# Order of the partial products in the projections: all sixteen matmuls with the weights' first parts, then the eight with the second parts

## The chip, the cores and the metric

The kernel runs on one core of a Trainium2 chip. The metric is the time of one execution on the device in microseconds (us). Five engines work at the same time, each through a queue of its own in order: TensorE (PE in the rows, its weight loads PEld), VectorE (DVE), ScalarE (ACT), GpSimd (POOL) and SyncE (SP), which here starts transfers.

## What is computed

Two layers of a decoder over 320 tokens (256 of a prompt, 64 of eight samples), model width 1024, all in fp32:

```python
for l in range(DEPTH):
    xn = rmsnorm(x)
    u = xn @ w_in[l]        # IN_WIDTH columns: pooling, its gate z, latents, q/k/v, their gates, 3 branch gates
    A = pool_mixer(...)     # windows 2, 4, 8, 16; mean minus token, then a linear map per group
    B = attention(...)      # latent, over cached pages
    C = gated_delta(...)    # short convolutions, then a chunked recurrence
    x += w_out( sum_b sigmoid(gate_b) * P_b(branch_b * silu(z_b)) )
```

(shortened). Nearly all of the work of TensorE is the product of `xn` with 128 columns of `w_in` at a time.

## The kernel before

Everything is stored with features on the partitions, so that one product gives 128 columns for all 320 tokens: eight steps k of 128 features each, added up in one PSUM tile.

**Three matmuls per step.** For precision each weight tile and `xn` are split in two parts. `split_w` has ScalarE round the weight tile to `wh` (L200) and VectorE, or in some turns GpSimd, subtract to get the rest `wl` (L201). `xn` has the parts `xnH` and `xnL`, made once per layer. A product is then `wh xnH + wh xnL + wl xnH`: 3 matmuls for each of 8 steps, 24 in all. `mm3` (L213 to L226) issues them. It has two forms: steps one after the other with the three matmuls of each together (L223 to L226), or first the sixteen matmuls that use `wh` (L218, L219) and then the eight that use `wl` (L221). Before the change the second form is taken only by the first two products of layer 0.

**Who calls it.** `proj` (L425 to L430) makes a product of the projections into a PSUM tile named `pj`, of which there are two. The rows name it `pj`; a thin product of 72 columns per layer is named `pj` as well. `gate_mm` (L456) makes those of the branch gates (`gate`); it always hands over a range of k, `ks`, which is `(0, 8)` unless a product is issued in pieces. Products of the branches (`br`) have four steps, those of the attention's queries three. The products with `w_out` (`wo`, L1544) have eight and hand over no range.

**Weights.** Raw tiles of 128 x 1024 values come from memory into four buffers (`wraw`); `wh` and `wl` have two buffers each, used in turns. So ScalarE can make the next `wh` when the last matmul that reads the buffer is done.

**Order.** Outside the attention the program is given to a scheduler that places the instructions of every engine by a model of their durations. So the order on VectorE, ScalarE and GpSimd is not that of the code, and moves when products are issued otherwise. Each engine then keeps that order.

**The stretches around the end of a layer's recurrence.** `pooling(g)` makes a product of the pooling branch, its sums `us` over windows (L642), the difference `d` (L646 to L649) and its linear map, a matmul into `mix` (L651); a transpose `pout` (L636) is taken from it as well. `pool_gate(g)` makes the product of its gate: `z` (L658), a tanh `th` (L660, L661). At the same time the delta rule runs on VectorE: a recurrence in seven rounds on `X8` and `R` (L764 to L766), from it three matrices `TS` (L772), which are transposed (L774) and then doubled up in levels: products `Y` (L797) on TensorE, copied by ScalarE (`Yb`, L800), products `Z` (L813), subtracted (L819) and transposed (L820) on VectorE. In layer 1 a logarithm and an exponential on ScalarE (L549, L550) stand behind the first `Yb`; VectorE needs them for `qq` (L552).

Of the kernel before, what the change touches and what calls it, by code (L numbers as in the profile page):

```python
# [36 lines left out]
PRM, RNB, STB, XT, WLP = "M", "M", "M", ("A", "B"), 2  # L37
# [79 lines left out]
def trunk(tc, I, O, layers=2):  # L117
# [66 lines left out]
    turn, hold, pair, paired = [0], [], [0], [1]  # L184
# [28 lines left out]
    def mm3(out, w, x, nk, first=0, ks=None):  # L213
        wh, wl = w
        xh, xl = x
        if l == 0 and turn[0] <= WLP:
            for k in range(nk):
                nc.tensor.matmul(out, wh[:, k, :], xh[:, first + k, :], start=k == 0, stop=False)  # L218
                nc.tensor.matmul(out, wh[:, k, :], xl[:, first + k, :], start=False, stop=False)  # L219
            for k in range(nk):  # L220
                nc.tensor.matmul(out, wl[:, k, :], xh[:, first + k, :], start=False, stop=k == nk - 1)  # L221
            return
        for k in range(*(ks or (0, nk))):  # L223
            nc.tensor.matmul(out, wh[:, k, :], xh[:, first + k, :], start=k == 0, stop=False)  # L224
            nc.tensor.matmul(out, wh[:, k, :], xl[:, first + k, :], start=False, stop=False)  # L225
            nc.tensor.matmul(out, wl[:, k, :], xh[:, first + k, :], start=False, stop=k == nk - 1)  # L226
# [187 lines left out]
    for l in range(layers):  # L414
# [10 lines left out]
        def proj(col):  # L425

            w = split_w(ahead.pop(0) if ahead else load_w(I["w_in"][l][:, col : col + 128], 8, 128), 8)
            b = ps(chunk.get("tag", "pj"), "pj")
            mm3(b[:, :T], w, xn, 8)
            return b[:, :T]  # L430
# [25 lines left out]
        def gate_mm(tag, w, b=None, ks=(0, 8)):  # L456
            b = b or ps(tag, "gate")
            mm3(b[:, :T], w, xn, 8, ks=ks)
            return b
# [102 lines left out]
        w = split_w(small, 8, lambda w: w[:, :, :72])  # L562
        bs = ps("pj", "pj")
        mm3(bs[:72, :T], [i[:, :, :72] for i in w], xn, 8)
        kr4 = per.tile([128, T], F32, name="kr4", tag="kr4")
        tt(kr4[0:32, :], bs[0:32, :T], rn[0:32, :], mult)
# [1041 lines left out]
```

## Time and profile before

| | before |
|---|---|
| median of 3 runs | 1044.32 us (1042.73 to 1047.79) |
| the profiled execution | 1044.8 us, of which the span from first to last instruction is 1042.8 |
| mean granted clock of TensorE | 0.973 of full |
| busy: TensorE | 987.6 us (95%) |
| busy: VectorE | 712.1 us (68%) |
| busy: ScalarE | 466.5 us (45%) |
| busy: GpSimd | 332.2 us (32%) |

The rest of the page is read best by stretches, since the shares of busy time differ between them. In the rows below, `x` behind a busy time is a number of instructions, and `[1.05 <-ACT wh L200]` behind an instruction says that its engine was idle for 1.05 us before it, and that the instruction of line 200 on ScalarE which wrote `wh` released it.

### The profile page before, as it was taken

Reading aid. Unit: us, or ns where it says so; the run is one execution under the profiler, and the core shown is the slowest. Engines: PE = TensorE matmul, PEld = TensorE weight load, DVE = VectorE, ACT = ScalarE, POOL = GpSimd, SP = SyncE. Lnnn points to the kernel's source line nnn. Section 1 sums busy time; section 2 is a strip of 40 time slices with the busy share of each in tenths; the row PEclk is TensorE's granted clock in tenths of the full one; section 3 lists DMA queues with packets and bytes.
Section 4 is the critical chain, followed back from the end, with each engine's and each line's share of the span. In section 5 each row is a group of like instructions: output and inputs, shape, how many; then the busy total and the mean of one; then the engine's idle time right before and its main releaser. Section 6 shows DMA issues by size and latency. Waiting matters only on the chain.

```text
span 1042.8 us, 24809 instructions
## 1 busy us (share of the span) xinstructions
PE 987.6 (95%) x10211; PEld 865.2 (83%) x10211; DVE 712.1 (68%) x1353; ACT 466.5 (45%) x838; POOL 332.2 (32%) x467
## 2 busy tenths in 40 slices
PE   8988899999999999999989979999999999998996
PEld 6877798997878888789978868999887787877996
DVE  3899974658656666677758988646774675754962
ACT  5554253555443333444546534336455333334453
POOL 3656312124250101035445542221334201100631
PEclk8999899999999999999999989999999999999999
DMA  9533324633656776268563333455256577633861
GB/s 235 158 82 101 96 74 111 184 96 91 203 171 202 242 233 225 78 196 233 144 194 94 86 98 82 109 144 140 71 145 232 163 227 259 189 135 126 237 171 51
DMA packets 202698, 159.22 MB, mean 153 GB/s; under 512 B 27704, under 2 KB 191826, under 8 KB 200010
## 3 DMA queue, kind: packets, MB, share of 16 engines
q1 hardware_dynamic: 176364, 98.47, 34.7%
q0 software_dynamic: 7424, 48.75, 13.2%
q10 hardware_dynamic: 18798, 10.44, 3.5%
q8 instruction: 80, 1.31, 0.5%
q14 instruction: 32, 0.26, 0.1%
HBM read 144.17 MB, written 13.68 MB: 151 GB/s over the span
## 4 chain that ended last, share of the span: by engine, by line
PE 73%; DVE 16%; ACT 5%; issue 3%; DMA 2%; POOL 1%; SPq 0%; DVEq 0%; ACTq 0%; POOLq 0%
PE sc L1186 6%; PE pv L1257 6%; PE pj L224 5%; PE gate L224 5%; PE pj L226 5%; PE pj L225 5%; PE gate L226 5%; PE gate L225 4%; DVE cy L509 4%; DVE wl L201 3%; PE br L226 3%; PE br L224 3%; PE br L225 3%; PE wo L224 2%; PE wo L225 2%
## 5 line engine op out<-in xcount | busy, mean ns | idle before, releaser
L201 DVE TENSOR_TENSOR wl<-wraw,wh 128x1024 fp32r<-128x1024 f32 (+2 forms) x169 | 195.9, 1167 | 83.0 <-ACT wh L200 82.0
L200 ACT ACTIVATE wh<-wraw 128x1024 fp32r<-128x1024 f32 (+1 forms) x180 | 166.5, 935 | 156.4 <-PE pj L225 75.8
L224 PE MATMUL pj<-xnH,wh 128*128 128x320 f32 (+1 forms) x528 | 172.7, 327 | 13.0 <-DVE V L501 7.6
L226 PE MATMUL pj<-xnH,wl 128*128 128x320 f32 (+1 forms) x528 | 170.2, 322 | 6.3 <-DVE wl L201 6.0
L225 PE MATMUL pj<-xnL,wh 128*128 128x320 f32 (+1 forms) x528 | 168.6, 319 | 0.0
L224 PE MATMUL gate<-xnH,wh 128*128 128x320 f32 x384 | 125.4, 326 | 1.7 <-DVE V L501 1.5
L226 PE MATMUL gate<-xnH,wl 128*128 128x320 f32 x384 | 121.2, 316 | 2.2 <-DVE wl L201 1.8
L225 PE MATMUL gate<-xnL,wh 128*128 128x320 f32 x384 | 120.1, 313 | 0.0
L224 PEld LDWEIGHTS pj<-xnH,wh 128*128 128x128 f32 (+1 forms) x528 | 101.8, 193 | 19.0 <-ACT wh L200 7.7
L226 PEld LDWEIGHTS pj<-xnH,wl 128*128 128x128 f32 (+1 forms) x528 | 101.7, 193 | 10.6 <-DVE wl L201 7.9
L225 PEld LDWEIGHTS pj<-xnL,wh 128*128 128x128 f32 (+1 forms) x528 | 101.7, 193 | 4.9 <-issue 3.5
L224 PEld LDWEIGHTS gate<-xnH,wh 128*128 128x128 f32 x384 | 73.4, 191 | 9.3 <-issue 5.7
L1176 DVE STREAM_TRANSPOSE KT<-kv 128x1024 f32<-128x1024 f32 x64 | 78.6, 1228 | 0.5
L226 PEld LDWEIGHTS gate<-xnH,wl 128*128 128x128 f32 x384 | 73.3, 191 | 4.0 <-DVE wl L201 2.6
L225 PEld LDWEIGHTS gate<-xnL,wh 128*128 128x128 f32 x384 | 73.5, 191 | 1.1 <-issue 0.8
L224 PE MATMUL br<-yH,wh 128*128 128x320 f32 x192 | 61.1, 319 | 3.0 <-ACT wh L200 2.6
L226 PE MATMUL br<-yH,wl 128*128 128x320 f32 x192 | 60.4, 316 | 1.8 <-DVE wl L201 1.8
L225 PE MATMUL br<-yL,wh 128*128 128x320 f32 x192 | 60.2, 314 | 0.0
L1186 PE MATMUL sc<-KT,q 32*64 32x256 f32 x2048 | 59.3, 377 | 0.0
L1257 PE MATMUL pv<-kv,PT 128*64 128x256 f32 x512 | 58.8, 382 | 0.2
L509 DVE SCALAR_TENSOR_TENSOR cy<-V,prm,cy 128x344 f32<-128x344 f32 x72 | 56.4, 802 | 0.5
L1186 PEld LDWEIGHTS sc<-KT,q 32*64 32x64 f32 x2048 | 45.8, 131 | 12.0 <-issue 5.7
(410 smaller groups left out, 2045.1 us busy)
## 6 DMA issues: line engine op xcount, KB each, us to landing
wraw<-in_w_in SPq DMA_DIRECT2D x114, 512.0 KB
wraw<-in_w_out SPq DMA_DIRECT2D x16, 512.0 KB
q<-q4d SPq DMA_DIRECT2D x64, 72.0 KB
gate<-gt ACTq DMA_DIRECT2D x28, 160.0 KB
gt<-gate POOLq DMA_DIRECT2D x28, 160.0 KB, 3.5
wraw<-in_w_br_pool SPq DMA_DIRECT2D x16, 256.0 KB
wraw<-in_w_br_dn SPq DMA_DIRECT2D x16, 256.0 KB
wraw<-in_w_br_mla SPq DMA_DIRECT2D x16, 256.0 KB
```

The costliest lines, as they stand in the source:

```text
L200: act(h, raw, AF.Copy)
L201: (nc.gpsimd.tensor_tensor if spare or turn[0] in K["lo"] else tt)(lo, raw, h.bitcast(F32), sub)
L224: nc.tensor.matmul(out, wh[:, k, :], xh[:, first + k, :], start=k == 0, stop=False)
L225: nc.tensor.matmul(out, wh[:, k, :], xl[:, first + k, :], start=False, stop=False)
L226: nc.tensor.matmul(out, wl[:, k, :], xh[:, first + k, :], start=False, stop=k == nk - 1)
L509: stt(y, V[:, j : j + 344], wj(j), y, mult, add)
L1176: nc.vector.transpose(v[:, a], kv[:, a * 1024 : a * 1024 + 1024].rearrange("p (i k c) -> p i k c", i=4, k=8))
L1186: nc.tensor.matmul(sc[64 * hf : 64 * hf + 64, g, :256], q4[r, k, :], krT[r, keys_] if k == 8 else KT[r, k, keys_], start=k == 0, stop=k == 8,)
L1257: nc.tensor.matmul(pv[64 * hf : 64 * hf + 64, :256], PT[:, n * 128 + 64 * hf : n * 128 + 64 * hf + 64], kv[:, r : r + 256], start=n == 0, ...
```

## The change

In `mm3` the condition under which the second form is taken becomes: eight steps, and no range of k handed over.

```diff
--- before.py
+++ after.py
@@ -213,7 +213,7 @@
     def mm3(out, w, x, nk, first=0, ks=None):
         wh, wl = w
         xh, xl = x
-        if l == 0 and turn[0] <= WLP:
+        if nk == 8 and not ks:
             for k in range(nk):
                 nc.tensor.matmul(out, wh[:, k, :], xh[:, first + k, :], start=k == 0, stop=False)
                 nc.tensor.matmul(out, wh[:, k, :], xl[:, first + k, :], start=False, stop=False)
```

The two forms make the same 24 matmuls. By the order of the changed program, the products that take the second form are all those named `pj` and the sixteen named `wo`; 82 products more than before. Those named `gate` hand over a range and keep the first form, and so do `br` and the attention's queries.

What TensorE's queue holds in layer 1 for the gate product of a pooling group (pj_7382), before. `pout_7266` is the transpose of the pooling product ahead of it, `wh_7378` and `wl_7379` are its weights:

```order
L224 MATMUL pj_7382<-xnH_113,wh_7378 128x320
L225 MATMUL pj_7382<-xnL_114,wh_7378 128x320
L636 MATMUL pout_7266<-cst_58,u_7264 128x128
L226 MATMUL pj_7382<-xnH_113,wl_7379 128x320
L224 MATMUL pj_7382<-xnH_113,wh_7378 128x320
L225 MATMUL pj_7382<-xnL_114,wh_7378 128x320
L226 MATMUL pj_7382<-xnH_113,wl_7379 128x320
```

And after, from the end of its first sixteen matmuls to the next product (pj_7286):

```order
L636 MATMUL pout_7266<-cst_58,u_7264 128x128
L221 MATMUL pj_7382<-xnH_113,wl_7379 128x320 x8
L651 MATMUL mix_7276<-d_7271,mixw_6292 128x320
L218 MATMUL pj_7286<-xnH_113,wh_7282 128x320
L219 MATMUL pj_7286<-xnL_114,wh_7282 128x320
L218 MATMUL pj_7286<-xnH_113,wh_7282 128x320
L219 MATMUL pj_7286<-xnL_114,wh_7282 128x320
```

All sixteen matmuls with `wh_7378` now stand ahead of the transpose, and the first one with `wl_7379` is the seventeenth, not the third. The mix follows directly on the product in both.

On VectorE at the same place the parts of `d_7271`, the input of that mix, stood together before, between rounds of the recurrence (`X8`, `R`):

```order
L646 SCALAR_TENSOR_TENSOR d_7271<-us_7269,U_7259 128x256
L647 SCALAR_TENSOR_TENSOR d_7271<-us_7269,U_7259 128x64
L766 TENSOR_TENSOR R_7145<-R_7145,X8_7148 128x20x2
L648 TENSOR_TENSOR d_7271<-us_7269,cst1_6413 128x16
L764 STREAM_SHUFFLE X8_7152<-R_7145 128x160
L649 TENSOR_TENSOR d_7271<-d_7271,U_7259 128x16
L765 TENSOR_TENSOR X8_7152<-X8_7152,a8_6603 128x20x3
L766 TENSOR_TENSOR R_7145<-R_7145,X8_7152 128x20x3
L764 STREAM_SHUFFLE X8_7156<-R_7145 128x160
```

After the change:

```order
L646 SCALAR_TENSOR_TENSOR d_7271<-us_7269,U_7259 128x256
L647 SCALAR_TENSOR_TENSOR d_7271<-us_7269,U_7259 128x64
L765 TENSOR_TENSOR X8_7148<-X8_7148,a8_6603 128x20x2
L658 TENSOR_TENSOR z_7407<-pj_7382,rn_112 128x320
L201 TENSOR_TENSOR wl_7491<-wraw_7488,wh_7490 128x1024
L648 TENSOR_TENSOR d_7271<-us_7269,cst1_6413 128x16
L766 TENSOR_TENSOR R_7145<-R_7145,X8_7148 128x20x2
L661 SCALAR_TENSOR_TENSOR th_7409<-th_7409,z_7407 128x320
L649 TENSOR_TENSOR d_7271<-d_7271,U_7259 128x16
```

The gate's `z_7407`, the weights `wl_7491` of a later product and the tanh's `th_7409` moved in between the parts of `d_7271`; before they stood some ten rows further on, behind more rounds. In layer 0 the same three kinds moved in the same way.

Further on in layer 1, VectorE's rows from the end of the recurrence to the two transposes L774, before (`U_7311`, `u_7316`, `us_7321` and `d_7325` belong to the next pooling group):

```order
L766 TENSOR_TENSOR R_7145<-R_7145,X8_7168 128x20x7
L772 TENSOR_TENSOR TS_7172<-R_7145,cst1_6413 128x512
L772 TENSOR_TENSOR TS_7175<-R_7145,cst1_6413 128x512
L772 TENSOR_TENSOR TS_7178<-R_7145,cst1_6413 128x256
L630 TENSOR_TENSOR U_7311<-pj_7286,rn_112 128x256
L631 TENSOR_TENSOR U_7311<-pj_7286,rn_112 128x8x8
L774 STREAM_TRANSPOSE TS_7172<-TS_7172 128x512
L634 TENSOR_TENSOR u_7316<-pj_7286,rn_112 128x128
L774 STREAM_TRANSPOSE TS_7175<-TS_7175 128x512
L201 TENSOR_TENSOR wl_7416<-wraw_7413,wh_7415 128x1024
```

And after:

```order
L766 TENSOR_TENSOR R_7145<-R_7145,X8_7168 128x20x7
L642 TENSOR_TENSOR us_7323<-us_7321 128x452
L772 TENSOR_TENSOR TS_7172<-R_7145,cst1_6413 128x512
L772 TENSOR_TENSOR TS_7175<-R_7145,cst1_6413 128x512
L772 TENSOR_TENSOR TS_7178<-R_7145,cst1_6413 128x256
L658 TENSOR_TENSOR z_7444<-pj_7419,rn_112 128x320
L646 SCALAR_TENSOR_TENSOR d_7325<-us_7323,U_7311 128x256
L647 SCALAR_TENSOR_TENSOR d_7325<-us_7323,U_7311 128x64
L201 TENSOR_TENSOR wl_7589<-wraw_7586,wh_7588 128x1024
L774 STREAM_TRANSPOSE TS_7172<-TS_7172 128x512
L774 STREAM_TRANSPOSE TS_7175<-TS_7175 128x512
```

The transposes had only parts of `U_7311` and `u_7316` ahead of or between them; now `wl_7416` and the first `us` (just ahead of these rows), the second `us`, `z_7444`, two parts of `d_7325` and `wl_7589` stand ahead of both.

TensorE's rows at that place, the products Y that read the transposed matrices, before:

```order
L797 MATMUL Y_7336<-TS_7172,ATm_7334 64x32 x14
L636 MATMUL pout_7318<-cst_58,u_7316 128x128
L797 MATMUL Y_7336<-TS_7172,ATm_7334 64x32 x2
L797 MATMUL Y_7357<-TS_7175,ATm_7355 64x32 x16
L226 MATMUL pj_7419<-xnH_113,wl_7416 128x320
L224 MATMUL pj_7419<-xnH_113,wh_7415 128x320
L225 MATMUL pj_7419<-xnL_114,wh_7415 128x320
```

And after, from the transpose `pout_7318` on:

```order
L636 MATMUL pout_7318<-cst_58,u_7316 128x128
L221 MATMUL pj_7419<-xnH_113,wl_7416 128x320 x8
L797 MATMUL Y_7336<-TS_7172,ATm_7334 64x32 x16
L797 MATMUL Y_7357<-TS_7175,ATm_7355 64x32 x7
L651 MATMUL mix_7330<-d_7325,mixw_6292 128x320
L797 MATMUL Y_7357<-TS_7175,ATm_7355 64x32 x9
L813 MATMUL Z_7450<-Yb_7353,TS_7172 64x32 x16
L813 MATMUL Z_7469<-Yb_7374,TS_7175 64x32 x16
```

Before, Y stood in the middle of the product pj_7419, with `pout_7318` between its parts; now the whole product and `pout_7318` stand ahead of it, and a mix between its parts.

## Rows read from the trace of the kernel before

**Rows 1.** Busy time by stretch: length; busy PE, PEld, DVE, ACT, POOL; PEclk; DMA share; GB/s

```profile
28.00:103.00 75.00, 66.28 (x457) 58.72 (x456) 69.06 (x121) 40.57 (x63) 47.28 (x73) 0.95 0.42 115
103.00:120.00 17.00, 13.09 (x67) 12.15 (x66) 16.21 (x47) 3.70 (x7) 6.32 (x9) 0.80 0.39 107
120.00:240.00 120.00, 118.36 (x1601) 108.37 (x1599) 75.56 (x144) 56.64 (x90) 27.92 (x40) 1.00 0.42 114
...
603.00:624.00 21.00, 14.81 (x80) 13.07 (x80) 18.80 (x48) 6.01 (x9) 10.05 (x13) 0.84 0.38 101
624.00:644.00 20.00, 17.76 (x202) 16.16 (x200) 17.19 (x31) 10.13 (x14) 4.98 (x6) 0.91 0.27 71
644.00:780.00 136.00, 135.24 (x1636) 120.81 (x1636) 88.11 (x169) 62.20 (x105) 36.36 (x46) 1.00 0.44 122
```

**Rows 2.** TensorE's waits over the whole span: us in total, times, longest

```profile
PE pj L224 <- DVE V L501: 7.6, 3, 3.1
PE pj L226 <- DVE wl L201: 6.0, 5, 2.3
PE pj L224 <- ACT wh L200: 3.1, 3, 1.1
...
PE gate L226 <- DVE wl L201: 1.8, 3, 1.1
```

**Rows 3.** Timeline of TensorE, layer 1, 612 to 624 us: start, length, instruction, idle before

```profile
613.37 0.41 PE L224 MATMUL pj<-xnH,wh 128*128 128x320 f32 x1 [1.05 <-ACT wh L200]
...
615.53 0.45 PE L636 MATMUL pout<-cst,u 128*128 128x128 f32 x1 [1.60 <-DVE u L634]
618.33 0.64 PE L226 MATMUL pj<-xnH,wl 128*128 128x320 f32 x1 [2.34 <-DVE wl L201]
618.76 0.47 PE L224 MATMUL pj<-xnH,wh 128*128 128x320 f32 x1
619.03 0.47 PE L225 MATMUL pj<-xnL,wh 128*128 128x320 f32 x1
...
622.90 0.31 PE L226 MATMUL pj<-xnH,wl 128*128 128x320 f32 x1
623.05 0.70 PE L651 MATMUL mix<-d,mixw 128*128 128x320 f32 x2
```

**Rows 4.** Timeline of TensorE, layer 0, 109 to 125 us

```profile
113.98 0.64 PE L226 MATMUL pj<-xnH,wl 128*128 128x320 f32 x1 [1.47 <-DVE wl L201]
...
119.87 0.70 PE L651 MATMUL mix<-d,mixw 128*128 128x320 f32 x2
...
124.03 1.18 PE L797 MATMUL Y<-TS,ATm 64*64 64x32 f32 x34
```

**Rows 5.** Timeline of VectorE, layer 0, 109 to 126 us

```profile
116.12 0.17 DVE L649 TENSOR_TENSOR d<-d,U 128x16 f32<-128x16 f32 x1
...
120.07 0.49 DVE L658 TENSOR_TENSOR z<-pj,rn 128x320 f32<-128x320 f32 x1 [0.49 <-PE pj L226]
```

**Rows 6.** The page's costliest groups: busy, mean ns of one, idle before

```profile
L201 DVE TENSOR_TENSOR wl<-wraw,wh 128x1024 fp32r<-128x1024 f32 (+2 forms) x169 | 195.9, 1167 | 83.0 <-ACT wh L200 82.0
...
L509 DVE SCALAR_TENSOR_TENSOR cy<-V,prm,cy 128x344 f32<-128x344 f32 x72 | 56.4, 802 | 0.5
```

**Rows 7.** Timeline of VectorE, layer 1, 614 to 645 us

```profile
616.43 0.61 DVE L642 TENSOR_TENSOR us<-U 128x454 f32<-128x454 f32 x1
...
619.71 0.17 DVE L649 TENSOR_TENSOR d<-d,U 128x16 f32<-128x16 f32 x1
...
629.66 0.69 DVE L774 STREAM_TRANSPOSE TS<-TS 128x512 f32<-128x512 f32 x1
...
631.38 1.74 DVE L642 TENSOR_TENSOR us<-U 128x454 f32<-128x454 f32 x1
...
638.23 1.70 DVE L552 TENSOR_TENSOR qq<-qq,l 128x320 f32<-128x320 f32 x4 [2.59 <-ACT l L550]
...
643.27 0.71 DVE L820 STREAM_TRANSPOSE TS<-TS 128x512 f32<-128x512 f32 x1
```

## The prediction

> **What bounds the kernel now.** I read busy time by stretch first, then the waits of TensorE, then the timelines of the places where those waits lie. In [rows 1] the reader is to compare PE and DVE in each row. From 28 to 120 us and from 603 to 644 us, the stretches in which layer 0 and layer 1 build their branches, VectorE is the fuller engine: 69.06 of 75, 16.21 of 17, 18.80 of 21 us. From 120 and from 644 us on TensorE is: 118.36 of 120 and 135.24 of 136. So there are two regimes. A wait of TensorE in the first is largely slack, since VectorE would still have to do the same work; only in the second does each microsecond of a product count fully, and there is next to no wait in it to remove.
>
> The list of waits [rows 2] gives those that the change can touch: 6.0 us, five times, for `wl` from VectorE, and 3.1 us, three times, for `wh` from ScalarE (which waits for the last reader of the buffer). Together 9.1 us, 0.9% of the span. The gates' 1.8 us stands there too. The timelines show where the long ones lie. In [rows 3] one product of layer 1 (pj_7382) waits 1.05 us for `wh`, starts, lets a transpose pass that waits 1.60, and then stands 2.34 us at its third matmul for `wl`. Its next matmuls start 0.27 us apart (618.76, 619.03), and the last start 0.15 us apart (622.90 to 623.05): the engine has been granted the lower of its two clock levels (1.2 instead of 2.4 GHz) after those idle pieces, which is what a granted clock of 0.84 and 0.80 in [rows 1] is made of. Layer 0 has the same picture [rows 4]: 1.47 us idle, and the product that started at about 110.7 reaches its end only at 119.87.
>
> **The change part by part.** The sum is made against the profiled execution, 1044.8 us (span 1042.8); the median of the runs is 1044.3, 0.5 below, and I forecast for the median.
>
> *What stays.* No instruction is added or removed; 82 products of 24 matmuls are issued in another order. At 0.15 us per matmul that is 82 x 24 x 0.15 us on either side: 0. The gates pass a range of k in any case, and the order of the changed kernel shows them as before. So the 1.8 us stay.
>
> *What a product gains.* `wl` is needed 14 matmuls later (17th instead of 3rd): 14 x 0.15 = 2.1 us. `wh` is released at the 16th instead of the 23rd: 7 x 0.15 = 1.0 us earlier. That covers four of the five `wl` waits and the three `wh` waits almost wholly, so the upper bound of the gain is 9.1 us, if TensorE were what the end of these stretches waits for. The lower bound is 0, because VectorE is nearer to full there. I take 0 for this term and judge the ends of the two stretches by themselves, since VectorE's order moves with the products.
>
> *End of the stretch in layer 0.* Before, `d` of the mix is ready at 116.12 + 0.17 = 116.3 [rows 5], and the mix stands at 119.87 behind the slow product. Now the product ends about 8 matmuls after its `wl`, near 115 to 116. But its `z` is now ready earlier too, and the scheduler has put `z` (0.49), the next product's `wl` (1.17, [rows 6]) and `th` (about as `z`) between the parts of `d`. With 0.3 of the recurrence that also steps ahead, `d` comes 2.4 us later: 118.7, and the mix at about 119.0, 0.9 earlier than 119.87. The product behind it (24 x 0.15 = 3.6) ends some 0.9 earlier as well, and Y, now at 124.03, by 0.9. But TensorE then idles 3 us in one piece ahead of the mix, where before it lost the clock after 1.47; if half of the next product runs at the lower level that is 12 x 0.12 = 1.4 us back. Bounds -0.9 and +1.4; I take -0.3, near the middle.
>
> *End of the stretch in layer 1.* The same move puts `z`, `wl` and `th` ahead of the last piece of `d`, which before ended at 619.9 [rows 7]: 2.1 us more, so the mix comes near 622.0 instead of 623.05, since its product is no longer late. Then comes the new queue: the two transposes L774, of which the second began at 629.66, now stand behind another `wl` (1.17), a `z` (0.49), two `us` (0.61 each as at 616.43, up to 1.74 as at 631.38), part of `d` (about 0.6) and one more `wl` (1.17). That is 4.6 to 6.9 us more ahead of them. Less the 0.3 by which the earlier product fills an idle piece of VectorE, L774 comes 4.3 us later. Behind it wait Y (TensorE), Yb, then Ln and Exp (ScalarE), then `qq` (L552), which began at 638.23. About 1 us of that chain goes, by my estimate, because a transpose (pout) no longer stands between the parts of Y. So `qq` begins near 641.5 and ends (1.70) near 643.2. But what VectorE used to do behind `qq` (`z`, `wl`, `th`, one pair of L819 and L820) is already done by then; only one pair is left (0.71, and a subtraction on 256 columns, about 0.4 by the 0.49 of `z` on 320), and the last L820 ends near 644.3, against 643.27 + 0.71 = 643.98. Half of the Y that follows needs only the first pair and can run ahead of it, which is worth what the 0.3 costs. So the wait moves from `wl` to Y and nothing is won. Bounds: -1.1 (that pair in no one's way) and +2.3 (both `us` at the long duration, 2 x 1.13). I take 0.
>
> *Other moves.* In layer 1 a convolution's V (L501) stands behind one more `cy` (0.80) and one more `wl` (1.17, [rows 6]), where TensorE already waits up to 3.1 us [rows 2]. In layer 0 a V stands about as much ahead. Bounds -1 and +2, opposite signs in the two layers: 0. The sixteen products of `w_out` lie in a stretch where no wait is listed: 0.
>
> Sum: -0.3 on 1044.8 is 1044.5, or **1044.0** for the median of the runs.
>
> On a rule of the Trainium skill (Perfetto Trace Analysis, Optimization Strategies): keep the matmul engine as full as the program allows, and where it idles waiting for others, work on those. By it all of the 9.1 us would be won and the time be 1035.2; the stretches of [rows 1] speak against it here, since the engine waited for is itself full there.
>
> **The rivals.** Within 0.5% (5.2 us) is about what a measurement of this kernel cannot tell from no change: 1039.1 to 1049.5.
>
> A, the forecast: waits go from `wl` and `wh` to the mix and to Y, the ends of the stretches stay. Own range 1041 to 1048.
>
> B, faster: TensorE was the laggard after all. VectorE is not quite full (5.9 us idle of 75 in the first row, 2.2 of 21 in layer 1), and if that idling is for TensorE's products, ending these up to 2.1 us sooner lets VectorE pass too. All of 9.1 gives 1035.2, half of it 1039.8; I take 1037. For it speak [rows 2] and 618.33 in [rows 3]; against it, that VectorE's queue moves with it and brings no less work.
>
> C, slower: the clock. The new idle pieces are longer in one (3 to 5 us ahead of the mix and of Y), and they lie nearer to the TensorE-bound stretches, so products there run at 0.27 instead of 0.15 per matmul: 24 x 0.12 = 2.9 us each. It decides from 1.8 products on (5.2 / 2.9); two give 1050.1, four 1055.9. For it speaks the slow product of [rows 3], after pieces of 1.05, 1.60 and 2.34; against it, that those pieces are there already and the level came back within eleven matmuls.
>
> The Trainium skill (TensorE: Matmul & The Clock Gate, What's actually happening) says that the throttled level is the default and that recent activity releases it; this trace agrees, with 0.27 and 0.15 us per matmul in one product. It would speak for C, if the idle total grew.
>
> D: VectorE's instructions change their partners. `us` takes 0.61 or 1.74 us in the same kernel; a moved order can put several of these at either value: 2 to 4 us either way, 1040 to 1048.
>
> The title speaks of gates. Were they changed too, up to 1.8 us more would go; the order shows that they are not.
>
> **How the numbers follow.** A 0.55, B 0.25, C 0.14, D 0.06. The range 1036.5 to 1050 leaves out the lower half of B (about 0.10) and the larger part of C (about 0.09). Faster by over 0.5%: nearly all of B, 0.24, and 0.01 of the rest: 0.25. Slower: C and 0.02 of A and D: 0.16. The same: 0.59.
>
> **What would show it.** In the profile of the changed kernel: TensorE's waits for `wl` in projections gone or under 1 us, the gates' wait still there; waits of 3 us and more of the mix (L651) for `d` (L649) in both layers; in layer 1 a wait of 3 to 5 us of Y (L797) for L774, L774 some 4 us later, and the last L820 within 1 us of its place. VectorE's busy time in the four stretches as before. If instead both TensorE-bound stretches begin 2 us and more earlier, B was right; if the granted clock behind 120 or 644 us falls below 0.97, C. I would be wrong in the step on layer 1 if `qq` were early and Y not late.

## The result: 1.2% slower

The changed kernel takes 1056.66 us (median of 4, 1055.19 to 1057.43) against 1043.53 us for the kernel before on the same chip: 1.0118 times, with a 95% interval of 1.0085 to 1.0150. The profiled execution has a span of 1054.5 us, 11.7 more than before. The forecast was 1044.0 with a range up to 1050.

The stretches of [rows 1] in the changed kernel, with the same columns:

```profile
28.00:103.00 75.00, 65.87 (x454) 59.25 (x453) 67.35 (x120) 40.40 (x61) 48.28 (x72) 0.93 0.40 111
103.00:120.00 17.00, 11.80 (x75) 11.03 (x74) 16.13 (x47) 6.20 (x9) 6.40 (x10) 0.94 0.48 127
120.00:240.00 120.00, 119.28 (x1574) 109.64 (x1572) 76.68 (x147) 55.13 (x87) 27.55 (x39) 0.98 0.42 114
...
603.00:624.00 21.00, 16.20 (x101) 14.47 (x99) 19.48 (x32) 8.87 (x15) 14.64 (x13) 0.98 0.46 126
624.00:644.00 20.00, 14.64 (x115) 12.87 (x117) 14.25 (x43) 4.28 (x8) 3.01 (x7) 0.76 0.30 80
644.00:780.00 136.00, 135.15 (x1661) 121.02 (x1659) 87.88 (x166) 63.83 (x104) 37.89 (x48) 0.98 0.40 109
```

From 624 to 644 us neither engine is full: TensorE works 14.64 us of 20 (before 17.76) at a granted clock of 0.76, and VectorE 14.25 (before 17.19). The two wait for each other in turn. And TensorE's waits, to be held against [rows 2]:

```profile
PE mix L651 <- issue: 6.7, 2, 3.9
PE oT L1111 <- DVE so L1004: 4.3, 2, 2.4
...
PE pj L218 <- DVE al L577: 3.9, 1, 3.9
PE Y L797 <- DVE TS L774: 3.9, 1, 3.9
...
PE pj L218 <- ACT wh L200: 2.1, 2, 1.7
...
PE pj L221 <- DVE wl L201: 1.9, 2, 1.2
...
PE gate L226 <- DVE wl L201: 0.9, 2, 0.5
```

The waits for `wl` went from 6.0 to 1.9 us and those for `wh` from 3.1 to 2.1. In their place stand 6.7 us ahead of the mixes, 3.9 ahead of Y, 3.9 for `al` (L577; 0.6 before), and 4.3 us at a place that no row of before named: `oT` (L1111), which waits for `so` at the end of each layer's delta rule. In the kernel before, `oT` waited for `zs` alone, and it still does so:

```profile
PE oT L1111 <- DVE zs L1112: 1.5, 2, 0.8
```

The wait for `al` lies ahead of 60 us and leaves no loss at 120 us in the sums that follow.

To see where the span grew, I kept a ledger: I added up TensorE's work in both traces (each matmul at its usual distance from the next in the trace of before) and compared the times at which the same amount is done. A positive number says that TensorE is that many us behind the kernel before, whose own time stands in the first column. The other columns are of kernels described below.

```
us of before   after   r1     r12    what lies ahead of this time
 120           +0.0   -2.5   -3.5   layer 0, branches and recurrence
 140           +2.1   -1.8   -2.8   layer 0, mix and Y
 260           +0.6   -2.6   -3.7   layer 0, rest of the delta rule
 300           +5.5   -2.6   -3.6   layer 0, end of the delta rule
 480           +3.9   -4.1   -5.2   layer 0, attention and gated branches
 500           +3.8   +1.2   -5.2   layer 0, first products of w_out
 600           +5.3   -0.3   -7.3   layer 1, branches
 640           +7.8   +2.0   -6.9   layer 1, mix, Y, qq
 760           +8.9   +4.4   -5.8   layer 1, rest of the delta rule
 800          +11.6   +4.4   -5.8   layer 1, end of the delta rule
1000           +9.9   +4.5   -7.6   layer 1, attention and gated branches
1040          +11.9   +8.5   -6.5   layer 1, w_out
```

Two places carry most of it: the ends of the delta rule (+4.9 and +2.7) and layer 1 around mix and Y (from +3.8 at 610 to +8.6 at 660). The forecast knew only the second, and gave it 0.

The end of the delta rule in layer 0 on ScalarE, changed kernel (timeline; ACTq is ScalarE's queue itself, here issuing transfers):

```profile
265.11 0.47 ACT L439 ACTIVATE th<-zs 128x320 f32<-128x320 f32 x1 [0.64 <-DVE zs L437]
269.76 5.19 ACTq L996 DMA_DIRECT2D q4d<-qlat  x8
275.05 0.47 ACT L439 ACTIVATE th<-zs 128x320 f32<-128x320 f32 x1 [9.47 <-DMA q4d<-qlat]
275.54 1.28 ACT L1103 ACT_TABLE_LOAD   x1
...
278.45 0.31 ACT L1104 ACTIVATE r<-r,epsc 128x20 f32<-128x20 f32 x1
```

What waited for it on VectorE of the changed kernel, in the same timeline:

```profile
278.80 1.49 DVE L1106 TENSOR_TENSOR ot<-ot,r 128x1280 f32<-128x1280 f32 x1 [2.75 <-ACT r L1104]
280.21 0.35 DVE L1004 SCALAR_TENSOR_TENSOR so<-scn,cst 128x64 f32<-128x64 f32 x2
```

and on TensorE:

```profile
280.48 1.42 PE L1111 MATMUL oT<-cst,ot 64*64 64x64 f32 x40 [1.92 <-DVE so L1004]
```

The logarithm and exponential of the output's norm (L1103, L1104) stand behind eight transfers of `q4d`, whose issuing takes 5.19 us, and behind a tanh. The scheduler put them there; in the kernel before they stood ahead of the transfers. `ot` (L1106) follows them at 278.80, and `oT` after that. In the kernel before, ScalarE and then TensorE read so at this place, and `oT` has no wait:

```profile
269.21 0.31 ACT L1104 ACTIVATE r<-r,epsc 128x20 f32<-128x20 f32 x1
269.45 5.18 ACTq L996 DMA_DIRECT2D q4d<-qlat  x8
...
277.80 1.38 PE L1111 MATMUL oT<-cst,ot 64*64 64x64 f32 x40
```

In layer 1 the changed kernel has only the exponential behind the eight transfers; the logarithm (779.88) runs ahead of them.

### The profile page after: what moved, and what is told of

Read it like the earlier page. It is cut to its first block, busy times and chain, and to the rows that moved or that the text cites. A ratio compares the mean times of both kernels' runs of the same rounds, so it can differ in the third digit from the quotient of the medians.

```text
span 1054.5 us, 24807 instructions
## 1 busy us (share of the span) xinstructions
PE 990.9 (94%) x10211; PEld 869.0 (82%) x10211; DVE 706.1 (67%) x1353; ACT 468.7 (44%) x838; POOL 336.6 (32%) x467
## 4 chain that ended last, share of the span: by engine, by line
PE 67%; DVE 15%; issue 5%; ACT 4%; DMA 2%; POOL 1%; ACTq 1%; SPq 0%; DVEq 0%; POOLq 0%
PE sc L1186 6%; PE pv L1257 5%; PE gate L224 5%; PE pj L218 5%; PE gate L226 4%; PE gate L225 4%; PE pj L221 4%; PE pj L219 4%; DVE wl L201 3%; DVE cy L509 3%; PE br L226 2%; PE br L224 2%; PE br L225 2%; PE wo L221 2%; PE wo L219 2%
## 5 line engine op out<-in xcount | busy, mean ns | idle before, releaser
L218 PE MATMUL pj<-xnH,wh 128*128 128x320 f32 (+1 forms) x544 | 175.9, 335 | 11.0 <-DVE V L501 4.1
L219 PE MATMUL pj<-xnL,wh 128*128 128x320 f32 (+1 forms) x544 | 172.6, 329 | 0.0
L218 PEld LDWEIGHTS pj<-xnH,wh 128*128 128x128 f32 (+1 forms) x544 | 108.3, 199 | 18.2 <-ACT wh L200 7.2
L225 PE MATMUL gate<-xnL,wh 128*128 128x320 f32 x384 | 119.0, 310 | 0.0
L219 PEld LDWEIGHTS pj<-xnL,wh 128*128 128x128 f32 (+1 forms) x544 | 108.3, 199 | 2.0 <-issue 0.4
L221 PE MATMUL pj<-xnH,wl 128*128 128x320 f32 (+1 forms) x544 | 97.5, 319 | 1.9 <-DVE wl L201 1.9
L221 PEld LDWEIGHTS pj<-xnH,wl 128*128 128x128 f32 (+1 forms) x544 | 84.9, 192 | 7.0 <-issue 3.7
```

## The experiments

The scheduler works from instructions that have the same names in both kernels: a product's 24 matmuls are made one after the other in either form. So a kernel can take its form from one and the order of its queues from the other. To each of the twelve kernels but r10 this was added; `ORDER` holds, for each engine, the numbers of its instructions in the order wanted, and each edge fixes only the place in the queue, not a wait:

```python
def queue_as(nc, tc):
    made = {i.name: i for i in nc.cur_bb.bb.instructions}
    how = mybir.DependencyInfo(mybir.DependencyClass.NoSync, mybir.DependencyReason.DATA)
    for steps in ORDER:
        n, last = 0, None
        for step in steps:
            n += step
            if last is not None:
                tc.add_manual_dep(made[f"I-{n}"], last, how, reason="order")
            last = f"I-{n}"
```

All times are ratios to the kernel before, run in turn on the same chip. A ratio of 0.001 is 1.05 us.

**r1: new form, old order.** `ORDER` is that of the kernel before.

> The changed kernel, with the queue of every engine held to the order of the kernel before (the 24 matmuls of a product keep their places in TensorE's queue and are only exchanged among these). Theory A, the loss comes from the order that the scheduler chose anew for the other engines: then this is as fast as the kernel before or faster by up to the 9.1 us of waits for wl and wh, 1034 to 1044 us. Theory B, the form of sixteen and eight matmuls itself costs: then it is as slow as the changed kernel, 1053 to 1058 us. Theory C, only both together cost: 1042 to 1046 us here and in the opposite kernel too.

Measured: 1.0058 (1.0037 to 1.0080), half of the loss, and neither A nor B. The ledger above tells why: up to 480 us r1 is 4.1 us ahead, as A says, and then it loses 5.3 us at the first products of w_out, and 4.0 more at those of layer 1. Between 600 and 760 us it loses 4.7 as well, where r12 below, with the same queues at that place, loses 1.5; the part on the clock, near the end, comes back to this. The timeline of TensorE in r1 there:

```profile
493.14 0.42 PE L218 MATMUL wo<-mgH,wh 128*128 128x320 f32 x1 [1.52 <-ACT mgH L209]
495.11 0.41 PE L219 MATMUL wo<-mgL,wh 128*128 128x320 f32 x1 [1.55 <-DVE mgL L210]
```

The old order issues eighteen matmuls of the first product and then eleven of the second, because in the old form eighteen matmuls need only the first six of the eight pieces of `mg`. In the new form the thirteenth already needs the seventh, which comes late.

**r2: old form, new order.** The reverse.

> The opposite: products in the form of the kernel before, with every engine's queue held to the order of the changed kernel. Theory A: as slow as the changed kernel, 1053 to 1060 us, with waits for wl on top since the order was made for products that need it late. Theory B: 1042 to 1046 us. Theory C: 1042 to 1046 us.

Measured: 1.0336 (1.0299 to 1.0373), far slower than the changed kernel. Theory A has the direction, and the size is missed by 20 us and more. In its list of waits the first row is that for `wl`, longer than in [rows 2], since the order was chosen for products that need `wl` late:

```profile
PE pj L226 <- DVE wl L201: 9.2, 7, 3.3
```

That is 3.2 us more than there. By the ledger 8 us of the loss lie ahead of 120 us and 12 between 610 and 650; what causes them was not followed further.

**r3 and r4: the changed kernel with the old order in one stretch.**

> The changed kernel with its own order, but at the ends of the delta rule in both layers (from 262 to 292 us and from 760 to 800 us of the changed kernel) the order of the kernel before: there the logarithm and exponential of the output's norm (L1103, L1104) stand ahead of the eight transfers of q4d on ScalarE's queue. By the ledger of the two traces TensorE fell behind by 4.9 us at the first of these places and by 2.6 at the second. Theory A: 7.5 us are regained, 1049 us (1047 to 1051). Theory B: nothing is regained, 1055 to 1058 us.

> The changed kernel with its own order, but in layer 1 from the first rounds of the recurrence to the second pair of Z (about 612 to 652 us of the changed kernel) the order of the kernel before: d, the transposes L774 and Y as they stood there. TensorE fell behind by 5 us in this stretch. Theory A: 5 us are regained, 1051.5 us (1049 to 1054). Theory B: nothing, 1055 to 1058 us. Should the lower clock behind long idle pieces be the cause and not the order, less than half would be regained.

Measured: r3 1.0051 (1.0030 to 1.0072), r4 1.0077 (1.0051 to 1.0104). Against 1.0118 that is 7.0 and 4.3 us regained, each with some 4 us of uncertainty from the two intervals. So r3's gain is clear by itself and r4's is not; that of the same stretch is clear from r3 to r9 below, 0.58%. In r3's ledger TensorE loses nothing between 260 and 300 us, nor between 760 and 800. Theory A holds at both places. In r3 ScalarE reads so at the end in layer 0:

```profile
272.20 1.28 ACT L1103 ACT_TABLE_LOAD   x1
...
275.12 0.31 ACT L1104 ACTIVATE r<-r,epsc 128x20 f32<-128x20 f32 x1
275.63 5.18 ACTq L996 DMA_DIRECT2D q4d<-qlat  x8
```

The transfers take as long to issue, but nothing that TensorE waits for is behind them, and its first `oT` waits no more. r3 put back the queues of all engines at the ends, TensorE's and VectorE's too. That the transfers are what counts there is read from the timelines; a kernel with these alone moved was not made.

**r5, r6, r7: one part of the new form, old order.** In r5 w_out gets a range of k and so keeps the old form; in r6 only w_out is changed; r7 is r5 with layer 0 alone:

```diff
 r5  -                mm3(b[:, :T], w, mg, 8)
     +                mm3(b[:, :T], w, mg, 8, ks=(0, 8))
 r6  -        if nk == 8 and not ks:
     +        if nk == 8 and not ks and (x is not xn or l == 0 and turn[0] <= WLP):
 r7  as r5, and
     -        if nk == 8 and not ks:
     +        if nk == 8 and not ks and l == 0:
```

> As r1 (every queue held to the order of the kernel before), with the new form in the projections alone; the sixteen products of w_out keep the old form. In r1 TensorE fell behind by 5.3 us at the first of them in layer 0 and by 4.0 in layer 1, each waiting for the last sums of the gated branches. If that is the form's own cost there, this kernel is 9.3 us faster than r1, at 0.9970 of the kernel before (0.995 to 0.9995). If r1 lost to something else, it stays near 1.005.

> The opposite part alone: the new form in the sixteen products of w_out, the old one in the projections, every queue held to the order of the kernel before. If the first of these products needs its late operands too early, 9.3 us are lost: 1.009 of the kernel before (1.006 to 1.011). Otherwise 1.000.

> The new form in the projections of layer 0 alone, every queue held to the order of the kernel before. In r1 TensorE stood 2.5 us ahead of the kernel before at 120 us and 4.1 us ahead at 480. If that gain is kept: 0.9960 of the kernel before (0.994 to 0.9985). If later waits take it back: 1.000.

Measured: r5 0.9943 (0.9920 to 0.9966), r6 1.0096 (1.0059 to 1.0132), r7 0.9962 (0.9939 to 0.9985). r6 and r7 are as expected, and r5 gains slightly more than its range (0.995 to 0.9995) allowed. The two parts together give 1.0038, next to r1's 1.0058. So the new form in the projections is worth 6.0 us as long as the other queues stay, two thirds of it in layer 0. (r5's profiled execution was the longest of its twelve, 1047.2 us against a median of 1040.2, so its rows size nothing here.)

**r8: is it the clock?** As r5, with twenty matmuls in TensorE's idle piece ahead of Y in layer 1, into Y's own tile, which Y then overwrites:

```diff
                 Y = ps("A", "Y")[:, :256].rearrange("p (h i) -> p h i", i=32)
+                for _ in range(20 if l == 1 and m == LEVELS[0] and t == 0 else 0):
+                    nc.tensor.matmul(Y.rearrange("p h i -> p (h i)"), xn[0][:, 0, :128], xn[0][:, 0, :256], start=True, stop=True)
```

> As r5, with twenty further matmuls of 128x256 in layer 1 ahead of the first Y, whose result is overwritten at once: they fill the 3.0 us in which TensorE waited there in r1 for the transposes L774. In r1 the matmuls behind that wait ran at 0.27 us each for 10 us, and the last product of the stretch ended 4.4 us later against the kernel before than the wait began. If the granted clock is what costs there, this kernel is 1.5 to 3 us faster than r5, and the rows behind the wait start 0.15 us apart. If the waits themselves cost, it is as fast as r5 or slower by up to 0.5.

Measured: 0.9951 (0.9929 to 0.9973), no gain over r5. But the filling did not keep the clock either, as TensorE's timeline in r8 shows (L793 are the filling matmuls, and lines from there on are two higher):

```profile
620.49 2.56 PE L793 MATMUL Y<-xnH 128*128 128x256 f32 x20
624.55 1.00 PE L799 MATMUL Y<-TS,ATm 64*64 64x32 f32 x28 [1.50 <-DVE TS L774]
...
628.24 0.47 PE L219 MATMUL pj<-xnL,wh 128*128 128x320 f32 x1
628.50 0.47 PE L218 MATMUL pj<-xnH,wh 128*128 128x320 f32 x1
```

2.56 us of work were added, 1.50 us of idle time were left, and the rows behind still start 0.27 us apart. So this run doesn't decide what the clock costs there; a kernel with the level kept up was not made.

**r9: both corrections of r3 and r4 together. r10: projections alone, nothing held** (r5's edit without `queue_as`).

> The changed kernel with its own order, but in all three of the stretches of r3 and r4 the order of the kernel before. If the two add up (7.0 and 4.3 us regained): 1.001 of the kernel before (0.9985 to 1.0035). What then still lies between this and 0.9943, which the projections' new form gives in the old order (r5), is what the new order costs elsewhere, some 7 us. If the stretches were only a place where one loss shows, the second correction adds nothing: 1.005.

> The new form in the projections alone, w_out in the old one, and nothing held: the scheduler orders the queues itself. Outside the products of w_out its order is that of the changed kernel row by row. So the losses at the ends and in the solve stay, and only the 1.8 us at w_out of layer 1 go: 1.010 of the kernel before (1.007 to 1.012). If the form in w_out was the cause of the loss: 0.995.

Measured: r9 0.9993 (0.9973 to 1.0013), r10 1.0090 (1.0055 to 1.0125). The two corrections add up; with them the changed kernel is no slower than before. And when the scheduler orders the queues, the projections alone bring 0.90% of the loss of 1.18%, which the intervals do not tell apart from the whole; the same edit gains 0.57% in the old order.

**r11 and r12: what the idea is worth.** r11 gives the gates the new form as well, in r5's order. r12 is the whole change; around w_out alone it takes the changed kernel's order, elsewhere the old one:

```diff
 r11 as r5, and
     -        if nk == 8 and not ks:
     +        if nk == 8 and (not ks or ks[1] - ks[0] == 8 and x is xn):
```

> As r5 (new form in the projections, old in w_out, every queue held to the order of the kernel before), and the 48 products of the gates that are issued whole take the new form as well. They waited 1.8 us for wl from VectorE and 0.4 from GpSimd before: 0.9923 of the kernel before, if that lies on the path (0.990 to 0.996); 0.9943 as r5, if it does not.

> The whole change (projections and w_out in the new form), every queue held to the order of the kernel before, except around the products of w_out of both layers, where the order is the changed kernel's: there TensorE takes twelve matmuls of each of the first two products and five of a third ahead of the first late sum, where the old order takes eighteen of one and eleven of the next. If r1 lost its 9 us because the old order suits only the old form there: as r5, 0.9943 to 0.998. If the new form itself loses at w_out: 1.003 to 1.006, as r1.

Measured: r11 0.9912 (0.9883 to 0.9941), 1037.54 us, the fastest; r12 0.9952 (0.9927 to 0.9978), 1039.37 us. Both beat both kernels. r12 settles w_out: with twelve, twelve and five matmuls of the first three products ahead of the late piece, the new form loses nothing there (the ledger's -5.2 at 480 and at 500). r11 is 3.2 us below r5, but their intervals overlap, so what the gates give is not settled. r12's waits of TensorE:

```profile
PE pout L636 <- DVE u L634: 5.4, 3, 3.3
PE pj L218 <- DVE V L501: 5.0, 3, 2.8
PE Y L797 <- DVE TS L774: 3.3, 1, 3.3
```

The waits for `wl` and `wh` in projections are off the top of the list, and others have grown where VectorE is the fuller engine: Y waits 3.3 us for L774.

## Why the prediction was wrong

**The step that failed is "Other moves ... 0".** I followed VectorE's order to the two places where TensorE had waited before, and took it that elsewhere the new order costs nothing. It cost most where no wait had been listed: at the ends of the delta rule, where ScalarE's order changed along with the others', 7.0 us (r3). A place without a wait in the profile of before can be one where the order is just right.

**End of the stretch in layer 1: the mechanism was right, the size was not.** Forecast 0, bounds -1.1 and +2.3; measured 4.3 (r4), and 4.8 by the ledger from 610 to 660 us. One reading was wrong from the start: VectorE was called the fuller engine up to 644 us, but from 624 to 644 [rows 1] has 17.76 us for TensorE and 17.19 for VectorE, so by the prediction's own measure that stretch is not VectorE's. TensorE's timeline in the changed kernel:

```profile
625.50 1.41 PE L651 MATMUL mix<-d,mixw 128*128 128x320 f32 x2 [3.94 <-issue]
...
629.11 0.47 PE L219 MATMUL pj<-xnL,wh 128*128 128x320 f32 x1
629.37 0.47 PE L218 MATMUL pj<-xnH,wh 128*128 128x320 f32 x1
...
639.56 2.30 PE L797 MATMUL Y<-TS,ATm 64*64 64x32 f32 x46 [3.86 <-DVE TS L774]
641.79 1.43 PE L651 MATMUL mix<-d,mixw 128*128 128x320 f32 x2
643.15 1.17 PE L797 MATMUL Y<-TS,ATm 64*64 64x32 f32 x17
```

and VectorE's:

```profile
625.24 0.16 DVE L649 TENSOR_TENSOR d<-d,U 128x16 f32<-128x16 f32 x1
...
631.85 0.42 DVE L630 TENSOR_TENSOR U<-pj,rn 128x256 f32<-128x256 f32 x1 [1.86 <-PE pj L221]
...
638.71 1.30 DVE L774 STREAM_TRANSPOSE TS<-TS 128x512 f32<-128x512 f32 x2
...
650.22 1.70 DVE L552 TENSOR_TENSOR qq<-qq,l 128x320 f32<-128x320 f32 x4 [2.89 <-ACT l L550]
...
652.29 0.71 DVE L820 STREAM_TRANSPOSE TS<-TS 128x512 f32<-128x512 f32 x1
```

TensorE came to this stretch 3.8 us behind (the ledger at 610), which has to be taken off. The last part of `d` stands at 625.24 against 619.71 in [rows 7], 1.7 later without that, and 2.1 was the forecast. The mix, 3.94 us idle before it, starts at 625.50, 0.1 us behind the end of `d`: the wait of 3 us and more that was forecast, though the row names no releaser. Then the working went wrong. The product behind the mix ran at 0.27 us per matmul for some 3 us, so VectorE waited 1.86 us for it at `U`, with the last rounds of the recurrence queued behind. That is a wait of VectorE in a stretch where I had let it be full. L774's second transpose so came 5.9 us later, not 4.3 (639.34 against 629.66, less 3.8). Y then ran at the low level too (granted clock 0.50 from 641 to 644 us) and had a mix of 1.43 us between its parts, where I had counted a microsecond gained. `qq` came 8.2 us later, not 3.3, and the last L820 5.2 later, not 0.3.

**What a product gains: taken as 0, bounds 0 to 9.1; 6.0 (r5).** "VectorE is nearer to full there" was too strong: it idled 5.9 us of 75 in [rows 1], and ending products earlier did let it pass, as rival B said. In the old order its mechanism holds for 6.0 of the 9.1 us. But the scheduler does not leave the order alone, and B had left that out.

**The clock, rival C,** is part of the layer 1 loss, as the rows at 0.27 us show, and of layer 0's: there the mix came at 119.50 after 2.80 idle (forecast 119.0), and the product behind it ended at 126.2, so that TensorE was 2.1 us behind at 140 (forecast -0.3, bounds -0.9 and +1.4); all but 0.6 of that was made good by 260. The clock has a part in the ends of the delta rule too: in the changed kernel it is 1.00 from 262 to 280 us and 0.67 from 280.5 to 291, behind the wait of `oT`, and the sixteen matmuls of L1127 take 5.34 us there, 3.98 before. The Trainium skill (TensorE: Matmul & The Clock Gate, What's actually happening) says that the engine is throttled unless it has been busy of late. The trace agrees: matmuls stand 0.27 us apart behind the idle pieces of 2.80 and 3.94 us and 0.15 ahead of them. r8 shows that 2.56 us of extra work in one idle piece didn't keep the level up.

C's own sign, a clock below 0.97 behind 120 or 644 us, did not come: it is 0.98 in both rows. By the ledger's method, an estimate from the two traces, TensorE idles 8.6 us more over the whole span, and its matmuls stand further apart by 3.3 us in sum. So the idle pieces are the larger part, and that 1056.66 lies near C's price for four products, 1055.9, is luck. How much of the 4.3 us of layer 1 is the clock and how much the queue stays open, since r4 put both back at once. r1 and r12 show that the clock can move this stretch without the queue: their instructions and queues are the same there, TensorE idles 6.3 us in r1 and 7.2 in r12, and yet r1 loses 2.4 us from 610 to 660 and r12 0.5, at granted clocks of 0.84 and 0.90.

**w_out: 0 by forecast.** In the changed kernel, with its own order, 2.0 us by the ledger in layer 1 and nothing in layer 0; near enough. Only r1 and r6 show what the form costs when the order does not follow: 9 to 10 us. (The prediction's remark that the title speaks of gates is a slip: it names the projections alone, and r11 is the kernel with the gates.)

**The sum, from the runs:** the whole change with a good order 0.9952 (r12); the new order brings it to 1.0118, 17.4 us. Of these 7.0 are the ends (r3) and 4.3 the stretch in layer 1 (r4). Between r9 and r12 another 0.41% (4.3 us) lies in the new order elsewhere, by the ledger in layer 0's branches and mix and at the start of layer 1; no run took these apart. What is left, 1.8 us, is within the intervals.

## What to carry to other kernels

When a scheduler orders the queues, an edit to one engine's instructions is two edits: the one in the code, and the new order of every other engine. Hold the order fixed to see what the first is worth, and compare all queues, also where the profile shows no wait, to see what the second costs. Here the edit was worth a gain of 0.5% and the order took 1.7%; and issuing eight transfers from an engine that also computes was 5 us of that engine's queue, so what stands behind them should be what nobody waits for.

## What was not expected of the hardware

The lower clock does not begin with the idle piece, and not always with the first matmul behind it. TensorE's timeline in r8, earlier in the same stretch:

```profile
610.77 0.30 PE L636 MATMUL pout<-cst,u 128*128 128x128 f32 x1 [3.34 <-DVE u L634]
...
611.78 0.31 PE L218 MATMUL pj<-xnH,wh 128*128 128x320 f32 x1
611.93 0.35 PE L219 MATMUL pj<-xnL,wh 128*128 128x320 f32 x1
612.08 0.47 PE L218 MATMUL pj<-xnH,wh 128*128 128x320 f32 x1
612.34 0.47 PE L219 MATMUL pj<-xnL,wh 128*128 128x320 f32 x1
```

After 3.34 us without work eight matmuls of the product behind the transpose start some 0.15 us apart, and only from 612.08 on they start 0.26 apart. The granted clock is 1.00 from 607.4 to 612.0 us, idle piece and eight matmuls, and 0.53 from 612.1 to 615.7. In layer 0 of the changed kernel it fell within the idle piece itself (0.71 from 116.7 to 119.5 us, 0.50 behind it). So the place where a product slows down need not be the place of the wait ahead of it.
